# A trunk layer on one core: the first two feed-forward sums taken over the un-normed residual, with the norm brought in where the sums are read

## The chip, the cores and the metric

The kernel runs on one core of a Trainium2 chip. The metric is the device time of one execution in microseconds, the median over a few runs. The profile shows one execution, with its engines named as follows: PE is TensorE's matmul, PEld its weight load, DVE is VectorE, ACT is ScalarE, POOL is GpSimd, SP is SyncE, which issues most of the transfers. "L138" is line 138 of the kernel. The kernel is written in program order: each engine takes its instructions in the order in which the Python code emits them, and waits for others by semaphores that are put in automatically.

## The reference

One layer of a diffusion backbone over 384 tokens (128 of context, 256 latent) of 2048 channels. Token mixing (attention, a Fourier branch, gates) ends in an output projection and a residual; then comes the feed-forward part with which the change deals:

```python
x = x + g1 * token_mixing(h, attn, u, w_na_proj_l, w_fnet_proj_l, w_gate_l, w_o_l)
h2 = rms_norm(x, n2) * (1 + sc2) + sh2
x = x + g2 * swiglu(h2, w_gu_l, w_down_l)

def swiglu(h, w_gate_up, w_down):
    a, g = jnp.split(h @ w_gate_up, 2, axis=-1)
    return (jax.nn.silu(g) * a) @ w_down
```

`rms_norm` divides each token by the root of its mean square over the 2048 channels, so it is one factor per token. `sc2` and `sh2` (scale and shift) are per channel, with one set for the context tokens and another for the latent ones. `D_FF` is 5632.

## The kernel before, in words

**Numbers in two parts.** All matrix products are of fp32 inputs, each split into a high part H, rounded to a shorter format by an ACT copy, and a low part L = x - H by a DVE subtraction (`split`, L135 to L138). `mm3` (L140 to L143) sums three products: H·H, H·L and L·H. So each weight tile costs one ACT cast (L137) and one DVE subtraction (L138).

**Weight units.** Weights stream in units of 256 rows by 512 columns (`load_unit`), issued on SP into four buffers `raw`. `next_unit` is called at the start of each unit's matmuls. It splits one further unit (`split_unit`, into buffers `wh` and `wl`, three of each), then lets the background work in the lists `front` and `behind` advance, starts a further load, and hands out a unit that was split two calls earlier. The split writes into the buffer of the unit just finished, so its cast begins when TensorE has left that unit.

**Background work.** A generator wrapped in `Paced` takes `rate` steps for each `next_unit`, after a delay of `wait` calls. Its instructions stand in the engines' queues behind those of the split in the same call. `rows` is such a generator: it sums the modulation rows of the later gates on DVE (L314), and its rate is set by stage (`RATES`).

**Accumulators.** Matmul outputs go to tiles of one bank in PSUM: four `mm` tiles and three `at` tiles. Sums take them in a ring of seven (`acc_tile`); transposes take an `at` tile.

**Output projection (W_o), L1122 to L1147.** Four chunks of 512 output channels. Each has three sums (one for each 128 tokens) over eight units. At its end x2 = xin + gate · sum is formed per token tile on DVE (L1142, L1143), and its squares are summed per token on ACT (L1145). While a chunk is computed, the chunk before it is turned to channels-first by `transposed` (L1107): for each 128 channels three TensorE transposes into an `at` tile, and two ACT passes that multiply by the scale and store to `x2T`, all in fp32.

**The seam, L1148 to L1187.** The last chunk's squares are summed, the inverse root is taken (`inv_sqrt`, L153), the shift columns `msh[1]` are finished (`rows_until(3)`, with a transpose at L347 and a copy at L351), the inverse is turned and spread over partitions (`rB`, L1157, L1159). `normed` (L1161) makes h2 in steps of two row groups of 128 channels: x2T · rB on DVE (L1165), the high part with the shift added on ACT (L1170), the low part on DVE (L1176). One step is taken ahead of the first feed-forward matmul, and the other seven go on one a unit; the last chunk is transposed in steps 2 to 5. The call of `next_unit` in the last W_o unit leaves out its split (`late`), which is done after the first `normed` step.

**Feed-forward part, L1212 to L1272.** Six parts of 8 or 4 blocks of 128 hidden channels. Per four blocks there are two sums over all 16 row groups, eight units each: first the gate half (`half` = 1), read by a Silu on ACT (L1241), then the linear half, multiplied in by DVE (L1244). The product is split into cH and cL for the down projection (L1251 to L1271), whose results are added up in `facc` until the last part writes y. The accumulators hold 384 tokens as columns, the weights being the stationary side.

Of the kernel before, what the change touches and what calls it, by code (L numbers as in the profile page):

```python
# [19 lines left out]
P = 128  # L20
# [75 lines left out]
def trunk_kernel(ctx: ExitStack, tc: tile.TileContext, io: dict):  # L96
# [28 lines left out]
    dram = ctx.enter_context(tc.tile_pool(name="dram", bufs=1, space=DRAM))  # L125


    small.tile([P, 56], F32, tag="pad", bufs=1, name="pad")

    ids = iter(range(10**9))  # L130

# [67 lines left out]
        for p in front:  # L199
            p.tick()  # L200

    def next_unit(late=False):

        for p in front:
            p.tick()
        if not late:
# [870 lines left out]
    rows_psum["tile"] = lambda: pmd.tile([P, CH], F32, tag="md8", name=nm("md"))  # L1077
    x2p = ctx.enter_context(tc.tile_pool(name="x2p", bufs=1))
    x2 = [x2p.tile([P, NT, CH], F32, tag=f"x2_{i}", name=f"x2_{i}") for i in range(4)]

    gb = [None] * 4

    def load_rows(pool, ty, cc):
        gb[cc] = pool.tile([P, 2, CH], F32, tag=f"gb{cc}", name=nm("gb"))
        for cnd in range(2):
            nc.sync.dma_start(
                gb[cc][:, cnd], s_row[ty][cnd][0, cc * CH : (cc + 1) * CH].partition_broadcast(P)
            )
            yield

    pho = ctx.enter_context(ExitStack())
    xtp = pho.enter_context(tc.tile_pool(name="xtp", bufs=1))
    tmp = pho.enter_context(tc.tile_pool(name="tmpo", bufs=2))
    x2T = [xtp.tile([P, 4, TOK], F32, tag=f"x2T{i}", name=f"x2T{i}") for i in range(4)]
    ssx = small.tile([P, NT, 4], F32, tag="ssx", bufs=1, name="ssx2")

    def load_residual(cc):

        nc.sync.dma_start(xin[cc][:, 0, :], xp[:, cc * CH : (cc + 1) * CH])
        yield  # L1100
        nc.sync.dma_start(
            xin[cc][:, 1:3, :], xs[:, cc * CH : (cc + 1) * CH].rearrange("(t p) d -> p t d", p=P)
        )
        rows_until(2)
        yield from load_rows(xtp, 2, cc)

    def transposed(cc):  # L1107

        for k in range(4):
            kt = cc * 4 + k  # L1110
            o = at_tile()
            for t in range(NT):
                nc.tensor.transpose(o[:, t * P : (t + 1) * P], x2[cc][:, t, k * P : (k + 1) * P], ident)
            for cnd, sl in ((0, slice(0, CTX)), (1, slice(CTX, TOK))):
                nc.scalar.activation(
                    out=x2T[cc][:, k, sl], in_=o[:, sl], func=AF.Copy, scale=msc[1][:, kt, cnd : cnd + 1]
                )
            yield

    rows.rate = RATES[3]  # L1120
    xin = [None] * 4
    for cc in range(4):  # L1122
        xin[cc] = xtp.tile([P, NT, CH], F32, tag="xin", bufs=2, name=nm("xin"))
        behind.append(Paced(load_residual(cc)))
        po = [acc_tile() for _ in range(NT)]
        for u in range(0, KT, 2):
            if cc == 3 and u == KT - 4:
                rows.rate = 0
            if cc == 3 and u == 8:
                warm_sqrt()  # L1130
            wH, wL = next_unit(late=cc == 3 and u == KT - 2)
            if u == 2 and cc:
                rows_until(4)
                behind.append(Paced(transposed(cc - 1)))
            for t in range(NT):
                sl = slice(t * P, (t + 1) * P)
                for kk in range(2):
                    k = u + kk
                    mm3(po[t], mixH[k][:, sl], mixL[k][:, sl], wH[:, kk], wL[:, kk], k == 0, k == KT - 1)
                if u == KT - 2:  # L1140
                    d = tmp.tile([P, CH], F32, tag="d", name=nm("d"))
                    nc.vector.tensor_mul(d, po[t], gb[cc][:, min(t, 1)])  # L1142
                    nc.vector.tensor_add(x2[cc][:, t], xin[cc][:, t], d)  # L1143
                    junk = tmp.tile([P, CH], F32, tag="junk", name=nm("junk"))
                    nc.scalar.activation(  # L1145
                        out=junk, in_=x2[cc][:, t], func=AF.Square, accum_out=ssx[:, t, cc : cc + 1]
                    )  # L1147
    ss2 = small.tile([P, NT], F32, tag="ss1", bufs=1, name="ss2")  # L1148
    nc.vector.tensor_reduce(out=ss2, in_=ssx, axis=AX.X, op=ALU.add)
    r2 = small.tile([P, NT], F32, tag="r1", bufs=1, name="r2")  # L1150
    for _ in inv_sqrt(r2, ss2, D, [P, NT]):
        pass
    rows_until(3)
    last_chunk = transposed(3)
    o = mm_tile()
    for t in range(NT):
        nc.tensor.transpose(o[:, t * P : (t + 1) * P], r2[:, t : t + 1].to_broadcast([P, P]), ident)  # L1157
    rB = tmp.tile([P, TOK], F32, tag="rB", bufs=1, name="rB")
    nc.scalar.copy(rB, o[:, :TOK])  # L1159

    def normed():  # L1161
        for k0 in range(0, KT, 2):
            for kt in (k0, k0 + 1):
                v = x2T[kt // 4][:, kt % 4]
                nc.vector.tensor_mul(v, v, rB)  # L1165
            for kt in (k0, k0 + 1):
                H, L = new_h(kt)
                v = x2T[kt // 4][:, kt % 4]
                for cnd, sl in ((0, slice(0, CTX)), (1, slice(CTX, TOK))):
                    nc.scalar.activation(  # L1170
                        out=H[:, sl], in_=v[:, sl], func=AF.Identity, bias=msh[1][:, kt, cnd : cnd + 1]
                    )
            for kt in (k0, k0 + 1):
                v = x2T[kt // 4][:, kt % 4]
                for cnd, sl in ((0, slice(0, CTX)), (1, slice(CTX, TOK))):
                    nc.vector.scalar_tensor_tensor(  # L1176
                        out=hL[kt][:, sl], in0=v[:, sl], scalar=msh[1][:, kt, cnd : cnd + 1],
                        in1=fr(hH[kt][:, sl]), op0=ALU.add, op1=ALU.subtract,
                    )
            if k0 in (2, 4, 6, 8):  # L1180
                next(last_chunk)
            yield

    norm = Paced(normed())
    norm.step()
    split_unit()
    behind.append(norm)  # L1187


    phf = ctx.enter_context(ExitStack())  # L1190
# [1 line left out]

    def split_act(i, sg, cH, cL):
        for f in range(4):
            split(cH[i + f], cL[i + f], sg[:, f])
            yield

    def gated():

# [1 line left out]
        phr.close()  # L1201
        pool = phr.enter_context(tc.tile_pool(name="gbp", bufs=1, side="right"))
        for cc in range(4):
            yield from load_rows(pool, 5, cc)
        for cc in range(4):
            for t in range(NT):
                v = facc[cc][:, t]
# [5 lines left out]
    for part, nf in enumerate(FF_PARTS):  # L1213
# [5 lines left out]
        for c4 in range(nf // 4):  # L1219
            for half in (1, 0):  # L1220
                po = [acc_tile() for _ in range(4)]
                for u in range(0, KT, 2):
                    wH, wL = next_unit()
                    if u == KT - 2 and facc is None:
                        norm.drain()
                        rows.rate = RATES[4]
                        pho.close()
                        actp = phf.enter_context(tc.tile_pool(name="actp", bufs=1))
                        facc = [actp.tile([P, NT, CH], F32, tag=f"fa{i}", name=f"facc{i}") for i in range(4)]
                        ftmp = phf.enter_context(tc.tile_pool(name="tmpf", bufs=2))  # L1230
                    for f in range(4):
                        s = slice(f * P, (f + 1) * P)
                        for kk in range(2):
                            k = u + kk
                            mm3(po[f][:, :TOK], wH[:, kk, s], wL[:, kk, s], hH[k], hL[k], k == 0, k == KT - 1)
                        if u < KT - 2:
                            continue
                        if half:
                            if f == 0:
                                sg = ftmp.tile([P, 4, TOK], F32, tag="sg", name=nm("sg"))  # L1240
                            nc.scalar.activation(out=sg[:, f], in_=po[f][:, :TOK], func=AF.Silu)  # L1241
                        else:
                            i = c4 * 4 + f
                            nc.vector.tensor_mul(sg[:, f], sg[:, f], po[f][:, :TOK])  # L1244
                            cH[i] = actp.tile([P, TOK], F32R, tag=f"cH{i}", name=nm("cH"))
                            cL[i] = actp.tile([P, TOK], F32R, tag=f"cL{i}", name=nm("cL"))
                            if nf == 4:
                                split(cH[i], cL[i], sg[:, f])
            if nf > 4:
                behind.append(Paced(split_act(c4 * 4, sg, cH, cL), 2))  # L1250
        for cc in range(4):  # L1251
            po = [acc_tile() for _ in range(NT)]
            for u in range(0, nf, 2):
                wH, wL = next_unit()
                for t in range(NT):
# [8 lines left out]
                    elif not last:  # L1264
                        nc.vector.tensor_add(facc[cc][:, t], facc[cc][:, t], po[t])
                    else:
                        d = ftmp.tile([P, CH], F32, tag="d", bufs=1, name=nm("d"))
# [57 lines left out]
```

## Time and profile before

| what | us |
|---|---|
| median of 3 runs | 2071.12 |
| lowest and highest run | 2070.62, 2074.38 |
| the profiled execution, its own time | 2071.76 |
| its span, first to last instruction | 2070.0 |
| TensorE busy in the span | 2035.2 |
| DVE busy | 1225.5 |
| ACT busy | 758.2 |

The page gives busy times over the whole span and per group of instructions; a "tile" name stands for all of its buffers. The views by stretch give the same for chosen times, with the clock that TensorE was granted, 1.00 being full speed; the mean over the span was 0.996. TensorE's busy time contains pipelined matmuls, so "busy" is not "at full rate": the distance from one matmul's start to the next is the better measure. In the timeline, a number in brackets is how long the engine stood idle before an instruction, and after the arrow is whose signal ended it.

### The profile page before, as it was taken

The numbers are of one execution on the slowest core, as the hardware profiler recorded it, in microseconds if no ns is written. First come the engines' busy times: TensorE is split into PE (matmuls) and PEld (weight loads), VectorE is DVE, ScalarE is ACT, GpSimd is POOL, SyncE is SP. The second block draws the span as 40 slices with busy tenths as digits, with TensorE's granted clock in tenths as the row PEclk, the third lists the DMA queues.
The fourth block names the chain that finished last, engine by engine and source line by source line (L and its number), as shares of the span: only waits on it lengthen the run. The fifth ranks groups of instructions, "written<-read, shape, count | busy, mean of one in ns | idle before, by whom it ended". The sixth has DMA issues, their size and how long they took to land.

```text
span 2070.0 us, 27406 instructions
## 1 busy us (share of the span) xinstructions
PE 2035.2 (98%) x10986; PEld 1846.1 (89%) x10986; DVE 1225.5 (59%) x1454; ACT 758.2 (37%) x1133; POOL 43.2 (2%) x92
## 2 busy tenths in 40 slices
PE   7999999999999999998999999999999999999999
PEld 4658888999999999887998899899989998999897
DVE  5635899688986787765554444544454434333456
ACT  5323232456665443334433332223222232223222
POOL 1000000000001000001000000000000000000000
PEclk9999999999999999999999999999999999999999
DMA  9887878677774775754545554455454444444453
GB/s 329 297 318 218 298 247 315 209 211 232 213 223 150 255 245 198 244 182 133 153 153 163 157 159 153 136 160 162 154 163 133 125 130 127 128 126 128 130 166 122
DMA packets 219999, 390.45 MB, mean 189 GB/s; under 512 B 28080, under 2 KB 64960, under 8 KB 219872
## 3 DMA queue, kind: packets, MB, share of 16 engines
q1 hardware_dynamic: 212704, 382.13, 58.2%
q10 hardware_dynamic: 4672, 6.31, 0.8%
q8 instruction: 86, 1.41, 0.3%
q0 software_dynamic: 2496, 0.27, 0.1%
q14 instruction: 41, 0.34, 0.0%
HBM read 371.81 MB, written 20.51 MB: 190 GB/s over the span
## 4 chain that ended last, share of the span: by engine, by line
PE 89%; DVE 3%; DMA 3%; ACT 2%; issue 1%; SPq 1%; ACTq 0%; DVEq 0%
PE mm L141 18%; PE mm L143 18%; PE mm L142 18%; PE at L143 11%; PE at L141 11%; PE at L142 10%; PE md L392 1%; DMA wm<-in_w_mod 1%; DVE accr L314 1%; DMA wraw<-in_w_gate 1%; DVE wl L138 1%; ACT wh L137 0%; ACT sc L900 0%; SPq L368 0%; PE at L858 0%
## 5 line engine op out<-in xcount | busy, mean ns | idle before, releaser
L138 DVE TENSOR_TENSOR wl<-wraw,wh 128x1024 fp32r<-128x1024 f32 (+1 forms) x464 | 559.1, 1205 | 699.9 <-ACT wh L137 693.5
L137 ACT CAST wh<-wraw 128x1024 fp32r<-128x1024 f32 (+1 forms) x464 | 480.6, 1037 | 1030.3 <-PE at L142 283.5
L141 PE MATMUL mm<-hH,wh 128*128 128x384 f32 x1216 | 411.6, 338 | 3.6 <-ACT gst L998 2.5
L143 PE MATMUL mm<-hH,wl 128*128 128x384 f32 x1216 | 407.6, 335 | 0.0
L142 PE MATMUL mm<-hL,wh 128*128 128x384 f32 x1216 | 407.2, 335 | 0.0
L314 DVE SCALAR_TENSOR_TENSOR accr<-wmr,csz,accr 128x1024 f32<-128x1024 f32 x240 | 304.7, 1277 | 0.1
L141 PE MATMUL at<-hH,wh 128*128 128x384 f32 x704 | 236.6, 336 | 1.4 <-ACT hH L1170 1.4
L141 PEld LDWEIGHTS mm<-hH,wh 128*128 128x128 f32 x1216 | 228.9, 188 | 9.2 <-ACT gst L998 3.7
L142 PE MATMUL at<-hL,wh 128*128 128x384 f32 x704 | 236.4, 336 | 0.0
L143 PE MATMUL at<-hH,wl 128*128 128x384 f32 x704 | 235.9, 335 | 0.0
L142 PEld LDWEIGHTS mm<-hL,wh 128*128 128x128 f32 x1216 | 229.0, 188 | 0.0
L143 PEld LDWEIGHTS mm<-hH,wl 128*128 128x128 f32 x1216 | 228.7, 188 | 0.0
L141 PE MATMUL mm<-wh,hH 128*128 128x512 f32 x422 | 168.8, 400 | 1.8 <-DVE gl L1054 1.2
L142 PE MATMUL mm<-wl,hH 128*128 128x512 f32 x422 | 165.0, 391 | 0.9 <-DVE wl L138 0.9
L143 PE MATMUL mm<-wh,hL 128*128 128x512 f32 x422 | 164.7, 390 | 0.0
L143 PE MATMUL mm<-wh,cL 128*128 128x512 f32 x352 | 137.1, 389 | 0.0
L141 PE MATMUL mm<-wh,cH 128*128 128x512 f32 x352 | 137.0, 389 | 0.0
L142 PE MATMUL mm<-wl,cH 128*128 128x512 f32 x352 | 137.0, 389 | 0.0
L141 PEld LDWEIGHTS at<-hH,wh 128*128 128x128 f32 x704 | 132.7, 189 | 2.8 <-ACT hH L1170 1.8
L142 PEld LDWEIGHTS at<-hL,wh 128*128 128x128 f32 x704 | 132.7, 189 | 1.1 <-DVE hL L1176 0.7
L143 PEld LDWEIGHTS at<-hH,wl 128*128 128x128 f32 x704 | 132.7, 189 | 0.0
L141 PEld LDWEIGHTS mm<-wh,hH 128*128 128x128 f32 x422 | 79.5, 188 | 33.7 <-issue 11.1
(239 smaller groups left out, 2390.2 us busy)
## 6 DMA issues: line engine op xcount, KB each, us to landing
wraw<-in_w_gate_up SPq DMA_DIRECT2D x176, 512.0 KB, 3.7
wmr<-in_w_mod SPq DMA_DIRECT2D x128, 512.0 KB, 4.2
wraw<-in_w_down SPq DMA_DIRECT2D x88, 512.0 KB, 3.7
wm<-in_w_mod SPq DMA_DIRECT2D x64, 512.0 KB, 7.1
wraw<-in_w_gate SPq DMA_DIRECT2D x64, 512.0 KB, 5.0
wraw<-in_w_in SPq DMA_DIRECT2D x56, 512.0 KB, 5.8
wraw<-in_w_o SPq DMA_DIRECT2D x32, 512.0 KB, 5.5
wraw<-in_w_fnet_proj SPq DMA_DIRECT2D x16, 512.0 KB, 6.2
```

Of the source, the lines that this page charges most:

```text
L137: nc.scalar.copy(H, x)
L138: nc.vector.tensor_sub(L, x, fr(H))
L141: nc.tensor.matmul(out, aH, bH, start=start, stop=False)
L142: nc.tensor.matmul(out, aH, bL, start=False, stop=False)
L143: nc.tensor.matmul(out, aL, bH, start=False, stop=stop)
L314: nc.vector.scalar_tensor_tensor(out=acc[:, cnd], in0=wm, scalar=sc, in1=acc[:, cnd], op0=ALU.mult, op1=ALU.add)
L392: nc.tensor.matmul(pm[q : q + 32, :w], csz[:, k, :], wm[:, ty, kk + par, :], start=k < 2, stop=k >= KT - 2, tile_position=(0, q), skip_gro ...
```

## The change

The first two feed-forward sums (gate and linear half of the first four blocks) no longer read h2 = x2 · scale · rB + shift. They read x2 · scale alone, with the norm factor rB and the shift brought in when the sums are read. This is possible since rB is one factor per token, that is, per column of the sum, and the shift's contribution is one number per output channel and condition.

- `transposed` now stores x2 · scale split into H and L (two ACT and two DVE passes for each row group) in `xw` (row groups 0 to 11) and `xv` (12 to 15). Their tiles are 386 columns wide: the last two hold the shift of the two conditions (`shifts`), so each sum's columns 384 and 385 come out as the shift's contribution. For this `rows_until(3)` now stands in the last W_o unit.
- The last W_o unit splits a further weight unit as all others do.
- The inverse norm (`inverse`), the transposes of the last chunk and `normed` are all background work in the two sums. `inverse` acts in U0 and U2 (units of these sums, counted from 0), the transposes in U1 to U4, `normed` at 1.25 row groups a unit from the fourth unit on. `normed` adds H and L back together, multiplies by rB and splits into hH and hL, the low part one step behind, for the sums from the third on.
- `late_norm` reads each of the eight accumulators: the two shift columns are copied by ACT, DVE multiplies by rB, and then ACT's Silu takes the shift as its bias (first sum), or DVE adds it and multiplies by the first sum's result (second sum).
- `rows` goes on after the second sum, and not in the last unit of the first. The down projection's tiles are allotted after the second sum too; cH and cL are allotted when they are split. Temporaries `d` and `xin` now serve both stages, and the gate rows `gb` of the projection share two buffers.

```diff
+    XW = TOK + 2
+    xw = [xhp.tile([P, 12, XW], F32R, tag=f"x{n}", name=f"x{n}") for n in "HL"]
...
+    def shifts(some, k0):
+        H, L = some
+        c = slice(k0, k0 + H.shape[1])
+        nc.scalar.copy(H[:, :, TOK:], msh[1][:, c])
+        nc.vector.tensor_sub(L[:, :, TOK:], msh[1][:, c], fr(H[:, :, TOK:]))
...
-            for cnd, sl in ((0, slice(0, CTX)), (1, slice(CTX, TOK))):
-                nc.scalar.activation(
-                    out=x2T[cc][:, k, sl], in_=o[:, sl], func=AF.Copy, scale=msc[1][:, kt, cnd : cnd + 1]
-                )
+            H, L = wide(kt)
+            conds = [(msc[1][:, kt, c : c + 1], sl) for c, sl in ((0, slice(0, CTX)), (1, slice(CTX, TOK)))]
+            for g, sl in conds:
+                nc.scalar.activation(out=H[:, sl], in_=o[:, sl], func=AF.Copy, scale=g)
+            for g, sl in conds:
+                nc.vector.scalar_tensor_tensor(
+                    out=L[:, sl], in0=o[:, sl], scalar=g, in1=fr(H[:, sl]), op0=ALU.mult, op1=ALU.subtract
+                )
...
-            wH, wL = next_unit(late=cc == 3 and u == KT - 2)
+            wH, wL = next_unit()
+            if cc == 3 and u == KT - 2:
+                rows_until(3)
+                shifts(xw, 0)
...
+    def inverse():
+        ss2 = small.tile([P, NT], F32, tag="ss1", bufs=1, name="ss2")
+        nc.vector.tensor_reduce(out=ss2, in_=ssx, axis=AX.X, op=ALU.add)
+        r2 = small.tile([P, NT], F32, tag="r1", bufs=1, name="r2")
+        for _ in inv_sqrt(r2, ss2, D, [P, NT]):
+            pass
+        yield
+        yield
+        o = at_tile()
+        for t in range(NT):
+            nc.tensor.transpose(o[:, t * P : (t + 1) * P], r2[:, t : t + 1].to_broadcast([P, P]), ident)
+        nc.scalar.copy(rB, o[:, :TOK])
...
+        vs = tmp.tile([P, 4, TOK], F32, tag="xin", name=nm("v"))
+        conds = ((0, slice(0, CTX)), (1, slice(CTX, TOK)))
+        for kt in range(KT + 1):
+            if kt < KT:
+                xH, xL = (fr(x[:, :TOK]) for x in wide(kt))
+                v = vs[:, kt % 4]
+                nc.vector.tensor_add(v, xH, xL)
                 nc.vector.tensor_mul(v, v, rB)
+                new_h(kt)
+                for c, sl in conds:
                     nc.scalar.activation(
+                        out=hH[kt][:, sl], in_=v[:, sl], func=AF.Identity, bias=msh[1][:, kt, c : c + 1]
                     )
+            if kt:
+                for c, sl in conds:
                     nc.vector.scalar_tensor_tensor(
+                        out=hL[kt - 1][:, sl], in0=vs[:, (kt - 1) % 4, sl], scalar=msh[1][:, kt - 1, c : c + 1],
+                        in1=fr(hH[kt - 1][:, sl]), op0=ALU.add, op1=ALU.subtract,
                     )
             yield
-    norm = Paced(normed())
-    norm.step()
-    split_unit()
-    behind.append(norm)
+    norm = Paced(normed(), 1.25, 3)
+    behind += [Paced(inverse()), Paced(transposed(3), 1, 1), norm]
...
+    def late_norm(o, sg, half):
+        b = small.tile([P, 2], F32, tag="bias", name=nm("bias"))
+        nc.scalar.copy(b, o[:, TOK:XW])
+        v = sg if half else tmp.tile([P, CH], F32, tag="d", name=nm("v"))[:, :TOK]
+        nc.vector.tensor_mul(v, o[:, :TOK], rB)
+        for c, sl in ((0, slice(0, CTX)), (1, slice(CTX, TOK))):
+            if half:
+                nc.scalar.activation(out=sg[:, sl], in_=v[:, sl], func=AF.Silu, bias=b[:, c : c + 1])
+            else:
+                nc.vector.scalar_tensor_tensor(
+                    out=sg[:, sl], in0=v[:, sl], scalar=b[:, c : c + 1], in1=sg[:, sl], op0=ALU.add, op1=ALU.mult
+                )
...
+                            xH, xL = wide(k) if facc is None else (hH[k], hL[k])
+                            mm3(
+                                po[f][:, : xH.shape[1]], wH[:, kk, s], wL[:, kk, s], xH, xL, k == 0, k == KT - 1
+                            )
...
+                        if facc is None:
+                            late_norm(po[f], sg[:, f], half)
...
+            if facc is None:
+                norm.drain()
+                rows.rate = RATES[4]
+                phx.close()
```

More of the change, by code (lines that the diff above doesn't have):

```diff
@@ L125, in trunk_kernel @@
     dram = ctx.enter_context(tc.tile_pool(name="dram", bufs=1, space=DRAM))
-    small.tile([P, 56], F32, tag="pad", bufs=1, name="pad")
+    small.tile([P, 24], F32, tag="pad", bufs=1, name="pad")
     ids = iter(range(10**9))
@@ L200, in mid_unit, with next_unit @@
             p.tick()
-    def next_unit(late=False):
+    def next_unit():
         for p in front:
             p.tick()
-        if not late:
-            split_unit()
+        split_unit()
         for p in front + behind:
@@ L1079, in trunk_kernel, with load_rows @@
     x2 = [x2p.tile([P, NT, CH], F32, tag=f"x2_{i}", name=f"x2_{i}") for i in range(4)]
+    tmp = ctx.enter_context(tc.tile_pool(name="tmpx", bufs=2))
     gb = [None] * 4
[L1083 to L1084 removed]
+    def load_rows(pool, ty, cc, tag, bufs):
+        gb[cc] = pool.tile([P, 2, CH], F32, tag=tag, bufs=bufs, name=nm("gb"))
         for cnd in range(2):
@@ L1089, in load_rows, with wide @@
             yield
+    XW = TOK + 2
+    phx = ctx.enter_context(ExitStack())
+    xhp = phx.enter_context(tc.tile_pool(name="xhp", bufs=1))
+    xw = [xhp.tile([P, 12, XW], F32R, tag=f"x{n}", name=f"x{n}") for n in "HL"]
+    xv = []
+    def wide(kt):
+        return [x[:, kt] for x in xw] if kt < 12 else [x[:, kt - 12] for x in xv]
+    def shifts(some, k0):
[3 more added lines that the diff above has]
+        nc.vector.tensor_sub(L[:, :, TOK:], msh[1][:, c], fr(H[:, :, TOK:]))
     pho = ctx.enter_context(ExitStack())
-    xtp = pho.enter_context(tc.tile_pool(name="xtp", bufs=1))
-    tmp = pho.enter_context(tc.tile_pool(name="tmpo", bufs=2))
-    x2T = [xtp.tile([P, 4, TOK], F32, tag=f"x2T{i}", name=f"x2T{i}") for i in range(4)]
+    tmpo = pho.enter_context(tc.tile_pool(name="tmpo", bufs=1))
     ssx = small.tile([P, NT, 4], F32, tag="ssx", bufs=1, name="ssx2")
@@ L1104, in load_residual @@
         rows_until(2)
-        yield from load_rows(xtp, 2, cc)
+        yield from load_rows(tmpo, 2, cc, "gb", 2)
     def transposed(cc):
@@ L1122, in trunk_kernel @@
     for cc in range(4):
-        xin[cc] = xtp.tile([P, NT, CH], F32, tag="xin", bufs=2, name=nm("xin"))
+        xin[cc] = tmp.tile([P, NT, CH], F32, tag="xin", name=nm("xin"))
         behind.append(Paced(load_residual(cc)))
@@ L1143, in trunk_kernel @@
                     nc.vector.tensor_add(x2[cc][:, t], xin[cc][:, t], d)
-                    junk = tmp.tile([P, CH], F32, tag="junk", name=nm("junk"))
+                    junk = tmpo.tile([P, CH], F32, tag="junk", name=nm("junk"))
                     nc.scalar.activation(
@@ L1147, in trunk_kernel @@
                     )
[L1148 to L1158, printed above, removed]
@@ L1159, in trunk_kernel @@
-    nc.scalar.copy(rB, o[:, :TOK])
-    def normed():
-        for k0 in range(0, KT, 2):
-            for kt in (k0, k0 + 1):
-                v = x2T[kt // 4][:, kt % 4]
+    pho.close()
+    xvp = phx.enter_context(tc.tile_pool(name="xvp", bufs=1))
+    xv += [xvp.tile([P, 4, XW], F32R, tag=f"v{n}", name=f"v{n}") for n in "HL"]
+    rB = xvp.tile([P, TOK], F32, tag="rB", name="rB")
+    shifts(xv, 12)
+    def inverse():
[10 more added lines that the diff above has]
+        nc.scalar.copy(rB, o[:, :TOK])
@@ L1194, in split_act @@
         for f in range(4):
+            cH[i + f], cL[i + f] = (
+                actp.tile([P, TOK], F32R, tag=f"c{n}{i + f}", name=nm(f"c{n}")) for n in "HL"
+            )
             split(cH[i + f], cL[i + f], sg[:, f])
             yield
+    def late_norm(o, sg, half):
[10 more added lines that the diff above has]
+                )
     def gated():
@@ L1203, in gated @@
         for cc in range(4):
-            yield from load_rows(pool, 5, cc)
+            yield from load_rows(pool, 5, cc, f"gb{cc}", 1)
         for cc in range(4):
@@ L1223, in trunk_kernel @@
                     wH, wL = next_unit()
[L1224 to L1230, printed above, removed]
                     for f in range(4):
@@ L1266, in trunk_kernel @@
                     else:
-                        d = ftmp.tile([P, CH], F32, tag="d", bufs=1, name=nm("d"))
+                        d = tmp.tile([P, CH], F32, tag="d", name=nm("d"))
                         nc.vector.tensor_mul(d, po[t], gb[cc][:, min(t, 1)])
```

31 lines of the change are left out of this document (9 added, 22 removed).

## The prediction

> **What bounds the kernel now.** First the page's busy table: TensorE is busy 98% of the span, so a change can only win where TensorE idles or runs slowly.
>
> ```profile
> PE 2035.2 (98%) x10986; PEld 1846.1 (89%) x10986; DVE 1225.5 (59%) x1454; ACT 758.2 (37%) x1133; POOL 43.2 (2%) x92
> ```
>
> Then the table by stretches across the seam between the output projection and the feed-forward part. Its columns are the stretch, its length, the busy time of PE, PEld, DVE, ACT and POOL, the granted clock, the DMA share and GB/s.
>
> ```profile
> 830.00:958.00 128.00, 128.00 (x586) 104.97 (x585) 80.40 (x77) 46.34 (x74) 5.33 (x11) 1.00 0.64 210
> 958.00:964.00 6.00, 2.42 (x12) 1.80 (x11) 3.85 (x12) 2.37 (x7) 0.00 (x0) 0.92 0.00 0
> 964.00:970.00 6.00, 4.65 (x16) 4.01 (x15) 4.92 (x9) 3.85 (x7) 0.00 (x0) 0.51 0.03 5
> 970.00:980.00 10.00, 9.59 (x57) 8.95 (x56) 7.77 (x16) 6.10 (x14) 0.00 (x0) 1.00 0.52 157
> 980.00:1040.00 60.00, 59.91 (x345) 58.95 (x344) 32.93 (x51) 26.84 (x45) 0.00 (x0) 1.00 0.51 158
> 1040.00:2030.00 990.00, 990.00 (x5270) 931.43 (x5269) 447.90 (x451) 292.49 (x329) 6.26 (x13) 1.00 0.48 144
> ```
>
> TensorE is full up to 958 and again from 980; between, it idles, and runs at a clock of 0.51. The timeline says for what; brackets give the idle time ahead of an instruction and what ended it.
>
> ```profile
> 951.05 0.39 PE L141 MATMUL mm<-wh,hH 128*128 128x512 f32 x1
> ...
> 955.13 0.39 PE L141 MATMUL mm<-wh,hH 128*128 128x512 f32 x1
> ...
> 958.05 0.69 DVE L1142 TENSOR_TENSOR d<-mm,gb 128x512 f32<-128x512 f32 x1
> ...
> 960.92 0.63 ACT L1145 ACTIVATE junk<-x 128x512 f32<-128x512 f32 x1 [0.70 <-DVE x L1143]
> ...
> 961.67 0.17 DVE L1149 TENSOR_REDUCE ss<-ssx 128x3 f32<-128x12 f32 x1 [0.85 <-ACT junk L1145]
> ...
> 962.08 0.20 ACT L157 ACTIVATE rss<-rsv 128x3 f32<-128x3 f32 x1 [0.43 <-DVE rsv L155]
> ...
> 963.13 0.90 PE L1157 MATMUL mm<-ident,r 128*128 128x128 f32 x3 [3.58 <-DVE r L162]
> ...
> 966.02 0.69 PE L141 MATMUL at<-hH,wh 128*128 128x384 f32 x1 [1.35 <-ACT hH L1170]
> ```
>
> A W_o unit takes 4.08 (first two rows), so the projection ends at 959.2. TensorE then waits for the inverse norm and the first normed row. I call the feed-forward units of 24 matmuls U0, U1, and so on: the first two sums are U0 to U15, the third starts with U16. ACT's weight casts mark them, about 0.2 after each unit's start:
>
> ```profile
> 1024.75 1.05 ACT L137 CAST wh<-wraw 128x1024 fp32r<-128x1024 f32 x1 [3.11 <-PE at L142]
> ...
> 1037.23 1.05 ACT L137 CAST wh<-wraw 128x1024 fp32r<-128x1024 f32 x1 [3.11 <-PE at L142]
> ...
> 1045.59 1.05 ACT L137 CAST wh<-wraw 128x1024 fp32r<-128x1024 f32 x1 [2.28 <-issue]
> ```
>
> Three units fill 12.48, so a steady one takes 4.16; U16 starts at 1037.05, U18 at 1045.4. From 959.2 to 1045.4 are 86.2 us for 18 units worth 74.9: 11.3 us of other things. Four groups of three transposes stay. Such a group stretches a W_o unit from 4.08 to 4.45:
>
> ```profile
> 868.58 1.05 ACT L137 CAST wh<-wraw 128x1024 fp32r<-128x1024 f32 x1 [2.77 <-PE at L143]
> ...
> 873.03 1.05 ACT L137 CAST wh<-wraw 128x1024 fp32r<-128x1024 f32 x1 [2.77 <-PE at L143]
> ```
>
> So 0.37 a group, 1.5 for four, and 0.5 at that rate for rB's three and the shift's one. **At most 9.3 us (0.45%) can be won.**
>
> **The change, part by part.** *The gap.* U0 needs only x2 without its norm and the shift columns, so the waits of 3.58 and 1.35 and the slow clock behind them go. The shift's transpose moves ahead of the last W_o unit, which starts at 955.1. Its input is issued on POOL at 949.34 and 0.5 later, and lands in time (at most 3.7 later):
>
> ```profile
> 949.34 0.99 POOL L340 DMA_DIRECT2D colr<-s_row x2 [1.88 <-DMA s_row<-row]
> ```
>
> ```profile
> DMA to landing us min/median/max: 2.0/2.8/3.7
> L1086 SPq DMA_DIRECT2D gb<-s_row x16: 338/464/929, 834.1 to 1984.9; - x16
> ```
>
> Behind that unit's weights (low part done 2.5 after its start, at 957.6, by the cast rows below) come three tiny operations of 0.2: columns ready at 958.2. The three x2 tiles follow, six DVE passes of 0.69: 962.3, ahead of U1's transposes at 963.4. SP's order stays. The row sums of type 5 restart 8 units (33 us) later and are first read near 1985: no cost; if they came late, DVE would pay 1.28 a step there.
>
> *386 columns.*
>
> ```profile
> L143 PE MATMUL mm<-hH,wl 128*128 128x384 f32 x1216 | 407.6, 335 | 0.0
> ...
> L143 PE MATMUL mm<-wh,cL 128*128 128x512 f32 x352 | 137.1, 389 | 0.0
> ...
> L143 PE MATMUL at<-AH,chanL 128*128 128x388 f32 x16 | 5.4, 340 | 0.0
> ```
>
> That is 0.4 ns a column from 384 to 512 and 1.2 from 384 to 388: two columns in 384 matmuls cost 0.3 to 1.0 us. I take 0.4 (units of 4.18), the longer lever.
>
> *In W_o* DVE makes 12 low parts of 0.79 under a full TensorE (DVE 80.4 of 128 busy). In its second chunk two of three `at` tiles hold sums, so the third is freed by DVE, behind a row sum, instead of ACT; TensorE may wait 0.3 in three units: 0 to 1 us, I take 0.3.
>
> *The helpers' ring.* This decides, I expect. Each unit of the two sums issues a weight cast (ACT) and low part (DVE), then 1.25 steps of the norm: add and multiply on DVE, two ACT passes, and the low part of the row before, two DVE passes. Before, in DVE's and in ACT's timeline:
>
> ```profile
> 975.74 1.58 DVE L1176 SCALAR_TENSOR_TENSOR hL<-x2T,msh,hH 128x128 fp32r<-128x128 f32 x4
> 978.38 1.23 DVE L138 TENSOR_TENSOR wl<-wraw,wh 128x1024 fp32r<-128x1024 f32 x1 [1.06 <-ACT wh L137]
> 979.53 1.02 DVE L1165 TENSOR_TENSOR x2T<-x2T,rB 128x384 f32<-128x384 f32 x2
> ```
>
> ```profile
> 972.50 1.04 ACT L137 CAST wh<-wraw 128x1024 fp32r<-128x1024 f32 x1
> 975.30 1.50 ACT L1170 ACTIVATE hH<-x2T,msh 128x128 fp32r<-128x128 f32 x4 [1.76 <-DVE x2T L1165]
> 976.71 0.71 ACT L1115 ACTIVATE x2T<-at,msc 128x128 f32<-128x128 f32 x2
> 977.32 1.04 ACT L137 CAST wh<-wraw 128x1024 fp32r<-128x1024 f32 x1
> ```
>
> Each queue keeps its order, so the work forms a ring: cast to low part 1.06, low part 1.15, add and multiply 1.02, over to ACT 0.07, two ACT passes 0.70 (half of 1.41), and only then the next cast: **4.00 us for a unit with one step**. Every fourth unit has two; the second adds 0.79 (half of 1.58) and 1.02: **5.81**. Four units of ring take 17.8, of TensorE 16.7, so the helpers lose 1.1 each time. Their cover is the weights' lead: unit n's cast serves n+2, 8.36 later, and is done with its low part in 2.29, so 6.1 us of lag are free. Beyond that TensorE waits.
>
> *One `at` tile in U1 and U2.* Two hold sums again; row 12's transposes, rB's and row 13's share the third. After x2 (962.3) come the square and the spare shift columns (1.0), U2's cast and low part (2.3), the small inverse (1.4, as from 961.67 to 963.1 before), U3's low part (1.2) and row 12's (0.8): the tile is free at 969.0, TensorE there at 968.0. rB's transposes and its ACT copy (0.5) then hold up row 13's. With rB's own 0.4 this costs 2.0.
>
> *Summing the ring.* U6 starts at 959.2 + 6 x 4.18 + 1.5 + 2.0 = 987.8; its cast is at 988.5, as row 15's passes lengthened the units before. U6 has two steps: U7's cast at 994.3, its ring done at 998.3. Then the late norm of the first sum: per accumulator a tiny ACT copy, a DVE multiply, two Silu passes. ACT and DVE don't read one accumulator at once, as the attention part shows:
>
> ```profile
> 529.93 0.37 ACT L875 ACTIVATE sc<-at,rq 128x128 f32<-128x128 f32 x1 [3.67 <-DVE sc L870]
> ...
> 1000.72 1.28 ACT L1241 ACT_TABLE_LOAD   x1
> ...
> 1036.36 0.56 DVE L1244 TENSOR_TENSOR sg<-sg,at 128x384 f32<-128x384 f32 x1
> ```
>
> ACT is held for 0.1 + table load 1.28 + Silu 0.70, then three times 0.25 + 0.58 + 0.70: 6.7 us (the copy as L157's 0.20, the multiply from the last row with its hand-over, Silu as the L1170 passes). U8's cast comes at 1005.0, 8.8 after its unit's start at 996.2: 2.7 us of stall at U10. From there the ring sets the pace: U8 and U9 4.00 each, U10 5.81, U11 to U13 4.00 each, U14 5.81, U15 4.00, to 1040.6. Then the late norm of the second sum, on DVE in front of the next weights: 0.25, four times 0.51 + 0.79, the last row's low part 0.79, the weights' 1.23. U18 can start at **1048.1**, though TensorE ended U17 at 1043.1. Against 1045.4 that loses **2.7 us**: the gain at the head is taken back.
>
> *The clock.* The last stall is 5.0 us. A shorter one dropped the clock before:
>
> ```profile
> 648.50 0.44 PE L141 MATMUL mm<-hH,wh 128*128 128x384 f32 x1 [2.20 <-ACT gst L998]
> ...
> 650.00:652.00 2.00, 2.00 (x8) 2.00 (x7) 0.00 (x0) 1.20 (x4) 1.24 (x3) 0.50 0.55 200
> 652.00:654.00 2.00, 2.00 (x13) 2.00 (x12) 1.79 (x2) 1.92 (x5) 1.71 (x5) 0.90 0.30 106
> ```
>
> After 2.20 idle TensorE ran at half speed until about 652.4, 3.9 after its restart; at the seam from 966.0 until about 970. I take 3.8 us at half speed, **1.9 lost** (0 to 1.9). After U10 a drop only uses up waits that the ring imposes later anyway. The Trainium skill, "TensorE: Matmul & The Clock Gate", Part 1, says that the clock drops after a whole idle window of about 3.4 us on a free-running grid. By it the 2.20 would not have dropped it, which the row at 650 contradicts; a 5.0 us stall would hold a whole window only about every second time, and the term would be an estimated 0.9.
>
> **Sum:** 2.7 + 0.3 (W_o) + 1.9 = +4.9 on the profiled run of 2071.76 (span 2070.0), which lies 0.6 above the median 2071.12: **2076.0 us**, 0.24% slower. A measurement of this kernel can tell about 0.2%, 4.1 us, from no change.
>
> **Rivals.**
> 1. *The ring with a warm clock, or a shorter ring.* Without the drop 2071.1 + 3.0 = 2074.1; if ACT's copy did not hold DVE either, three hand-overs of 0.8 would go, 2071.7. Against: the rows at 529 and 650. For: each 1% of a 60 us ring is 0.6. Not measurable.
> 2. *Faster: the lead covers it.* If casts overlapped the norm's passes, DVE's work a unit (1.15 + 1.25 x 1.81 = 3.4) would stay under 4.18, and TensorE would keep 9.3 less 1.6 (the `at` tile) and 0.7 (columns, W_o): 7.0, 2064.1. It turns where the ring's mean falls below 4.18; I have 4.45. For: DVE was busy only 32.93 of 60 after 980. Against: the casts at 972.50 and 977.32, 4.82 apart, are such a ring.
> 3. *The gap stays in part:* U0 or row 12 still waits, though shift columns and x2 have margins of about 1 us. A miss of 2 gives 2078.0.
>
> **How the numbers follow.** Forecast 0.50, rival 1 0.32, rival 2 0.13, rival 3 0.05. The range leaves out rival 2 and the far end of 3: 2069 to 2080. Faster by over 0.2% 0.13, within 0.32, slower 0.55.
>
> **What would show it.** Right: no wait for r or hH near 959; short waits at rB's and row 13's transposes; waits for weight low parts (L138) at U10 and, near 5 us, at U18, with a clock near 0.5 behind it; casts 4.0 and 5.8 apart. Wrong: U16 reached near 1030 with the casts still waiting for TensorE, or a wait at U18 under 2 us.

## The result, and the profile after

The changed kernel takes 2075.05 us (median of 16 runs, 2073.54 to 2076.95), the kernel before in the same comparison 2070.90 (16 runs, 2068.51 to 2074.38). The ratio is **1.0021, with a 95% interval of 1.0014 to 1.0028: 4.2 us slower**, just at the 0.2% that I had named as the limit of what can be told, but with a sign that the interval settles. The forecast was 2076.0 with a range of 2069 to 2080.

The profiled execution of the changed kernel took 2074.58, with a span of 2072.8, which is only 2.8 more than the span before. That pair of spans understates it, since the two executions reach the changed part at different times. In ACT's timeline, the cast that follows a pair of casts at the start of W_o can serve as a mark that both kernels have, and the cast of U19, the second of the steady units behind the seam, as the end. Before:

```profile
831.53 1.06 ACT L137 CAST wh<-wraw 128x1024 fp32r<-128x1024 f32 x1 [0.87 <-ACT wh L137]
...
1049.71 1.05 ACT L137 CAST wh<-wraw 128x1024 fp32r<-128x1024 f32 x1 [3.06 <-PE mm L142]
```

After:

```profile
829.96 1.06 ACT L137 CAST wh<-wraw 128x1024 fp32r<-128x1024 f32 x1 [0.86 <-ACT wh L137]
...
1052.87 1.05 ACT L137 CAST wh<-wraw 128x1024 fp32r<-128x1024 f32 x1 [3.06 <-PE mm L142]
```

From mark to U19 it took 218.18 before and takes 222.91 after: **4.7 us more inside the changed stretch**, and the mark itself came 1.57 earlier in that execution, ahead of anything discussed here. Below, "after the mark" is a time counted from there; the same is done for each experiment.

The table by stretches of the changed kernel, with the columns of the prediction's:

```profile
958.00:964.00 6.00, 6.00 (x36) 5.81 (x35) 4.04 (x8) 3.32 (x8) 0.00 (x0) 1.00 0.32 89
964.00:970.00 6.00, 5.05 (x30) 4.52 (x30) 4.71 (x11) 3.39 (x7) 0.00 (x0) 1.00 0.53 146
...
980.00:1040.00 60.00, 54.15 (x301) 52.55 (x299) 42.52 (x78) 27.08 (x56) 0.00 (x0) 0.99 0.35 98
1040.00:1060.00 20.00, 18.94 (x96) 18.94 (x97) 14.19 (x25) 7.40 (x14) 0.00 (x0) 0.85 0.58 207
```

The hole between 958 and 970 is gone, with its slow clock. Another one has opened later: between 980 and 1040 TensorE is busy 54.15 of 60, and from 1040 the clock is 0.85. TensorE's timeline says for what it waits there:

```profile
1004.15 0.34 PE L143 MATMUL at<-xH,wl 128*128 128x386 f32 x1
1005.17 0.44 PE L141 MATMUL mm<-xH,wh 128*128 128x386 f32 x1 [0.68 <-ACT wh L137]
...
1006.43 0.44 PE L143 MATMUL mm<-xH,wl 128*128 128x386 f32 x1 [0.64 <-DVE wl L138]
...
1041.06 0.69 PE L141 MATMUL mm<-hH,wh 128*128 128x384 f32 x1 [4.80 <-DVE v L1234]
...
1046.03 0.37 PE L141 MATMUL mm<-hH,wh 128*128 128x384 f32 x1
...
1048.69 0.33 PE L141 MATMUL at<-hH,wh 128*128 128x384 f32 x1
```

The waits of 0.68 and 0.64 are U10's, and both releasers are the weight split. The one of 4.80 is in U16, the first unit of the third sum, and its releaser is the late norm of the second sum (L1234). At 1046.03 the full speed is back (below). The last row is U18's first matmul. ACT's timeline shows what made the split late:

```profile
996.81 0.80 ACT L1203 ACTIVATE hH<-v,msh 128x128 fp32r<-128x128 f32 x2 [2.35 <-DVE v L1200]
997.52 0.14 ACT L1232 COPY bias<-at 128x2 f32<-128x2 f32 x1
...
1003.38 0.80 ACT L1237 ACTIVATE sg<-sg,bias 128x128 f32<-128x128 f32 x2 [0.62 <-DVE sg L1234]
1004.09 1.03 ACT L137 CAST wh<-wraw 128x1024 fp32r<-128x1024 f32 x1
1007.47 0.81 ACT L1203 ACTIVATE hH<-v,msh 128x128 fp32r<-128x128 f32 x2 [2.35 <-DVE v L1200]
1008.18 1.03 ACT L137 CAST wh<-wraw 128x1024 fp32r<-128x1024 f32 x1
...
1012.27 1.03 ACT L137 CAST wh<-wraw 128x1024 fp32r<-128x1024 f32 x1
...
1017.38 0.80 ACT L1203 ACTIVATE hH<-v,msh 128x128 fp32r<-128x128 f32 x2 [0.92 <-DVE v L1200]
1018.09 1.03 ACT L137 CAST wh<-wraw 128x1024 fp32r<-128x1024 f32 x1
```

From 997.52 to 1004.09 the first late norm holds ACT. From 978 until the second late norm no cast waits for TensorE any more. Outside the late norm each stands behind an `hH` pass, which waited for DVE (2.35 in a single step): casts come 4.09 apart with one norm step between them, and 5.82 with two. ACT is busy 27.08 of 60 here, and DVE 42.52: neither is full, and yet the pair of them sets the pace. DVE's end of it, at the second sum's late norm:

```profile
1039.45 0.74 DVE L1208 SCALAR_TENSOR_TENSOR hL<-v,msh,hH 128x128 fp32r<-128x128 f32 x2
1040.45 0.56 DVE L1234 TENSOR_TENSOR v<-mm,rB 128x384 f32<-128x384 f32 x1 [0.25 <-ACT bias L1232]
...
1046.12 1.22 DVE L138 TENSOR_TENSOR wl<-wraw,wh 128x1024 fp32r<-128x1024 f32 x1
```

The first multiply there starts at 1040.45, only when the ring has let go of DVE and, 0.25 later, of ACT, whose bias copy stood behind the last `hH` pass. It frees the accumulator at which TensorE stands. The last row is the low part of U18's weights: done at 1047.34, some 1.3 before TensorE gets there.

### The profile page after: what moved, and what is told of

It is laid out like the page before. It is cut to its first block, busy times and chain, and to the rows that moved or that the text cites. A ratio compares the mean times of both kernels' runs of the same rounds, so it can differ in the third digit from the quotient of the medians.

```text
span 2072.8 us, 27495 instructions
## 1 busy us (share of the span) xinstructions
PE 2037.9 (98%) x10986; PEld 1847.2 (89%) x10986; DVE 1247.5 (60%) x1516; ACT 760.8 (37%) x1147; POOL 43.3 (2%) x92
## 4 chain that ended last, share of the span: by engine, by line
PE 89%; DVE 4%; ACT 2%; DMA 2%; issue 1%; SPq 1%; ACTq 0%; DVEq 0%
PE mm L141 19%; PE mm L142 18%; PE mm L143 18%; PE at L143 10%; PE at L141 10%; PE at L142 10%; PE md L391 1%; DMA wm<-in_w_mod 1%; DVE accr L313 1%; DVE wl L138 1%; ACT wh L137 1%; PE at L857 1%; PE at L925 0%; SPq L181 0%; PE at L947 0%
## 5 line engine op out<-in xcount | busy, mean ns | idle before, releaser
L138 DVE TENSOR_TENSOR wl<-wraw,wh 128x1024 fp32r<-128x1024 f32 (+1 forms) x464 | 559.3, 1206 | 682.7 <-ACT wh L137 681.6
L141 PE MATMUL mm<-hH,wh 128*128 128x384 f32 x1152 | 390.4, 339 | 7.8 <-DVE v L1234 4.8
L143 PE MATMUL mm<-hH,wl 128*128 128x384 f32 x1152 | 386.0, 335 | 0.0
L142 PE MATMUL mm<-hL,wh 128*128 128x384 f32 x1152 | 385.8, 335 | 0.0
L142 PEld LDWEIGHTS mm<-hL,wh 128*128 128x128 f32 x1152 | 216.8, 188 | 0.0
L143 PE MATMUL at<-hH,wl 128*128 128x384 f32 x640 | 214.2, 335 | 0.0
L141 PE MATMUL at<-hH,wh 128*128 128x384 f32 x640 | 214.2, 335 | 0.0
L142 PE MATMUL at<-hL,wh 128*128 128x384 f32 x640 | 214.2, 335 | 0.0
L141 PEld LDWEIGHTS at<-hH,wh 128*128 128x128 f32 x640 | 120.4, 188 | 0.2
L142 PEld LDWEIGHTS at<-hL,wh 128*128 128x128 f32 x640 | 120.4, 188 | 0.2
L143 PEld LDWEIGHTS at<-hH,wl 128*128 128x128 f32 x640 | 120.4, 188 | 0.0
```

Of the source, the lines that this page charges most:

```text
L138: nc.vector.tensor_sub(L, x, fr(H))
L141: nc.tensor.matmul(out, aH, bH, start=start, stop=False)
L142: nc.tensor.matmul(out, aH, bL, start=False, stop=False)
L143: nc.tensor.matmul(out, aL, bH, start=False, stop=stop)
```

## The experiments

My theory: the helpers' ring (weight cast on ACT, low part, add and multiply on DVE, high part on ACT, next cast), together with the late norm in the same two queues, falls behind TensorE and hands back what the seam had won. Rivals: the 386 columns, the `at` tiles, the clock after the stall, or DVE simply having too much work. Experiments 1 to 4 share runs of the kernel before (2071.33, 22 runs), and 5 to 8 others (2070.99, 23 runs); with the 2070.90 of the first comparison these differ by 0.4, so the difference of two medians from separate comparisons is uncertain by about as much. All start from the changed kernel.

### 1. The high part one step behind

```diff
+            if kt:
                 for c, sl in conds:
                     nc.scalar.activation(
-                        out=hH[kt][:, sl], in_=v[:, sl], func=AF.Identity, bias=msh[1][:, kt, c : c + 1]
+                        out=hH[kt - 1][:, sl], in_=vs[:, (kt - 1) % 4, sl], func=AF.Identity,
+                        bias=msh[1][:, kt - 1, c : c + 1],
                     )
-            if kt:
```

> The high part of each normed row is written one step later too, beside its low part, so that ACT's two passes stand right behind the weight cast and wait for nothing, and the next cast no longer waits for DVE's multiply. Ring theory: the casts again start when TensorE leaves a unit (4.2 us apart), the waits near 1005 and 1019 go, DVE reaches the second sum's first accumulator about 8 us earlier and the 4.8 us wait at the third sum's first unit shrinks below 1 us; time about 2065.5 (2063 to 2068), 9 to 10 below the changed kernel and 5 below the one before. Rival (the 386 columns, the late norm's own work or a slower DVE and ACT cost the time, not the order of the queues): same amount of work, so it stays within 2 us of 2075.

Measured: **2065.01** (5 runs, 2063.77 to 2066.39), ratio 0.9968 [0.9956, 0.9981]. The two waits that TensorE has between 955 and 1062, and its row for the stretch that had the hole:

```profile
PE at L1129 <- ACT rB L1189: 0.6, 1, 0.6
PE at L1188 <- DVE vL L1135: 0.4, 1, 0.4
```

```profile
980.00:1040.00 60.00, 60.00 (x342) 60.00 (x341) 51.14 (x97) 33.81 (x70) 0.00 (x0) 1.00 0.40 112
```

ACT's and DVE's timelines in one of these units:

```profile
1017.99 1.05 ACT L137 CAST wh<-wraw 128x1024 fp32r<-128x1024 f32 x1 [0.98 <-ACT hH L1204]
...
1019.07 0.80 ACT L1204 ACTIVATE hH<-v,msh 128x128 fp32r<-128x128 f32 x2
1019.61 1.22 DVE L138 TENSOR_TENSOR wl<-wraw,wh 128x1024 fp32r<-128x1024 f32 x1
```

The high part now starts right behind the cast, with no wait, since its input was made a step before, and DVE's low part of the weights doesn't wait either. The work is the same, and DVE does more of it in the stretch than in the change (51.14 busy for 42.52), under a full TensorE. So DVE did not have too much to do: it was the order that made two engines with time to spare take turns. There is little room to spare, though: behind the first late norm DVE shows no idle time from 1003.61 to 1022.5 while it catches up. By the medians this one move is worth 10.0 us against the changed kernel, and makes it 0.32% faster than the kernel before.

### 2. The low part in its own step

```diff
-            if kt:
+            if kt < KT:
                 for c, sl in conds:
                     nc.vector.scalar_tensor_tensor(
-                        out=hL[kt - 1][:, sl], in0=vs[:, (kt - 1) % 4, sl], scalar=msh[1][:, kt - 1, c : c + 1],
-                        in1=fr(hH[kt - 1][:, sl]), op0=ALU.add, op1=ALU.subtract,
+                        out=hL[kt][:, sl], in0=v[:, sl], scalar=msh[1][:, kt, c : c + 1],
+                        in1=fr(hH[kt][:, sl]), op0=ALU.add, op1=ALU.subtract,
                     )
```

> Undoes one part: each low part stands in the step of its own row again, behind the high part that it needs. Ring theory: a unit with one step stays at 4.09 (the low part is done before the next cast is), a unit with two steps grows from 5.8 to about 6.6, since the second add waits for the first low part and that for ACT; three such units, so U16 and the time come 2.4 us later, 2077.5 (2076 to 2079). Rival (DVE's and ACT's amount of work decides): no difference, 2075.

Measured: 2077.66 (6 runs, 2076.82 to 2079.41), ratio 1.0029 [1.0018, 1.0041]. A double step in ACT's timeline:

```profile
1012.90 1.03 ACT L137 CAST wh<-wraw 128x1024 fp32r<-128x1024 f32 x1
1016.28 0.80 ACT L1203 ACTIVATE hH<-v,msh 128x128 fp32r<-128x128 f32 x2 [2.35 <-DVE v L1200]
1018.70 0.80 ACT L1203 ACTIVATE hH<-v,msh 128x128 fp32r<-128x128 f32 x2 [1.62 <-DVE v L1200]
1019.41 1.03 ACT L137 CAST wh<-wraw 128x1024 fp32r<-128x1024 f32 x1
```

The second `hH` pass waits 1.62 instead of 0.92, and the double step takes 6.51 instead of 5.82; a single one stays at 4.10. So the ring is lengthened by 0.7 in each fourth unit, which is 2.1 in the three double steps. TensorE's restart in U16 comes 213.5 after the mark for the change's 211.1, and the time follows, by 2.6. The part of the change that puts the low part a step behind does help; it is the other pass, the high part, that closes the ring.

### 3. The bias copy on DVE

```diff
-        nc.scalar.copy(b, o[:, TOK:XW])
+        nc.vector.tensor_copy(b, o[:, TOK:XW])
```

> The copy of the two shift columns in the late norm goes from ACT to DVE, so that ACT's Silu passes of one accumulator run beside DVE's multiply of the next. Ring theory: ACT is held 4.2 instead of 6.6 us behind the first sum, the wait near 1005 goes, the whole ring behind it and the second sum's late norm come 2.4 us earlier, and the wait at the third sum shrinks from 4.8 to about 2.4: time 2072 (2070.5 to 2073.5). Rival (ACT and DVE may read one accumulator at once, the hand-over costs nothing): 2075 to 2075.5.

Measured: 2073.12 (11 runs, 2071.67 to 2074.87), ratio 1.0009 [1.0000, 1.0017], 1.9 less than the change. ACT's timeline at the first late norm:

```profile
997.54 0.80 ACT L1203 ACTIVATE hH<-v,msh 128x128 fp32r<-128x128 f32 x2 [2.35 <-DVE v L1200]
...
999.64 2.88 ACT L1237 ACTIVATE sg<-sg,bias 128x128 f32<-128x128 f32 x8
1002.43 1.03 ACT L137 CAST wh<-wraw 128x1024 fp32r<-128x1024 f32 x1
```

The eight Silu passes run without a break, and the cast follows the `hH` pass by 4.89 instead of 7.28: 2.4 less, as worked out. Besides the 0.4 and 0.6 near 969, which stay, the list of TensorE's waits has only these two left:

```profile
PE mm L141 <- DVE v L1234: 4.6, 1, 4.6
PE mm L143 <- DVE wl L138: 0.5, 1, 0.5
```

The waits at U10 are gone; the 0.5 is U13's. But the one at U16 stayed at 4.6, where I had expected 2.4: TensorE, no longer held at U10, came to that point 2.4 earlier after the mark, and the late norm that it waits for there came 2.6 earlier (208.5 after the mark, for 211.1). The late norm pushes the whole ring back, wherever TensorE then pays for it.

### 4. No shift columns

The matmuls read 384 columns, and the bias is taken from the sum's first two, so this kernel leaves the shift out of its first two sums.

```diff
-        return [x[:, kt] for x in xw] if kt < 12 else [x[:, kt - 12] for x in xv]
+        return [x[:, kt, :TOK] for x in xw] if kt < 12 else [x[:, kt - 12, :TOK] for x in xv]
...
-        nc.scalar.copy(b, o[:, TOK:XW])
+        nc.scalar.copy(b, o[:, 0:2])
```

> Leaves out the shift in the first two sums: the matmuls read 384 columns instead of 386, and the bias copy reads two other columns of the same accumulator, so every wait stays. Ring theory: TensorE saves 0.3 to 1.0 us in units that wait for the ring anyway, so the time stays within 0.7 of the changed kernel, 2075. Rival (386 columns, not a multiple of 32, are read or written slowly): 2 us or more are saved, 2073 or less.

Measured: 2074.89 (11 runs, 2072.56 to 2077.64), ratio 1.0018 [1.0009, 1.0027]. That can't be told from the change. The columns do slow TensorE a little: 133 matmuls in a row take 23.39 from first to last start after, 0.1772 each, and 23.22 without the columns, 0.1759 each. In TensorE's timeline, first and last of the 133 after,

```profile
979.70 0.33 PE L143 MATMUL at<-xH,wl 128*128 128x386 f32 x1
...
1003.09 0.34 PE L143 MATMUL at<-xH,wl 128*128 128x386 f32 x1
```

and without the columns:

```profile
979.69 0.34 PE L143 MATMUL at<-xH,wl 128*128 128x384 f32 x1
...
1002.91 0.34 PE L143 MATMUL at<-xH,wl 128*128 128x384 f32 x1
```

That is 0.5 us in 384 matmuls. While the ring sets the pace it is waited away: no difference shows in the time.

### 5. Experiments 1 and 3 together

> Both edits of the runs e1 and e3 together. Ring theory: a hand-over between ACT and DVE costs only inside the ring; with the ring broken no wait for weights is left for it to shorten, so the time stays with e1, 2065.0 (2064 to 2066). Rival (the hand-overs cost 1.9 by themselves, as e3 gained): 2063.

Measured: 2064.92 (6 runs, 2062.78 to 2067.31), ratio 0.9971 [0.9959, 0.9983]: the same as experiment 1. The copy on ACT cost 1.9 while the ring was closed, and nothing that can be measured once it is open.

### 6. rB's transposes in their own bank, on top of experiment 1

```diff
-        o = at_tile()
+        o = rows_psum["tile"]()
```

> The edit of e1, and the transposes of the inverse norm go to the bank of the row sums, which rest at that time, so that they no longer share the one free accumulator bank with rows 12 and 13. Theory (one bank in the first units costs two waits): the waits of 0.4 and 0.6 us near 969 go, 1 us less than e1, 2064.0 (2063 to 2065). Rival (those waits are covered by slack later): 2065.

Measured: 2064.52 (6 runs, 2063.09 to 2065.92), ratio 0.9970 [0.9957, 0.9982]. The two waits of experiment 1, 1.0 together, are gone from the trace: TensorE has none left between 950 and 1062. By time the step from experiment 1, 0.5, isn't separable from nothing, since the intervals overlap almost wholly.

### 7. The wait at U16 filled with matmuls

22 further matmuls into a bank at rest, in front of the fourth accumulator's first matmul in U16. They keep TensorE busy in front of the wait and add nothing to the sums.

```diff
+                            if part == 0 and c4 == 1 and half and k == 0 and f == 3:
+                                extra = rows_psum["tile"]()
+                                for _ in range(22):
+                                    nc.tensor.matmul(extra[:, :TOK], wH[:, kk, s], xH, start=True, stop=True)
```

> The changed kernel with 22 extra matmuls (3.8 us, into the resting bank of the row sums, read by nobody) in front of the matmul that waits 4.8 us in U16, so that TensorE idles there only about 1 us. Clock theory: the clock stays at full speed behind the wait; half of what the drop costs (16 matmuls at 0.32 instead of 0.17, 2.3 us) comes back, since U18's weights come at 1047.4 anyway where TensorE now starts U18 at 1048.5: 1.2 us less, 2073.8 (2073 to 2074.7). Rival 1 (the drop costs its full 2.3): 2072.7. Rival 2 (the clock does not matter behind this wait): 2075.

Measured: 2073.84 (10 runs, 2071.82 to 2075.02), ratio 1.0014 [1.0004, 1.0023]. By time alone that overlaps with the change; the trace tells them apart. Its timeline and, behind it, its table by stretches:

```profile
1037.73 3.98 PE L1277 MATMUL md<-hH,wh 128*128 128x384 f32 x22
1042.71 0.44 PE L141 MATMUL mm<-hH,wh 128*128 128x384 f32 x1 [1.00 <-DVE v L1234]
...
1048.03 0.33 PE L141 MATMUL at<-hH,wh 128*128 128x384 f32 x1
...
1049.04 0.44 PE L143 MATMUL at<-hH,wl 128*128 128x384 f32 x1 [0.50 <-DVE wl L138]
```

```profile
1041.00:1045.00 4.00, 3.00 (x18) 2.68 (x17) 3.67 (x10) 1.98 (x7) 0.00 (x0) 1.00 0.46 131
```

The same stretch of the changed kernel, which lies at its restart:

```profile
1036.00:1041.00 5.00, 0.26 (x2) 0.00 (x0) 3.57 (x7) 2.65 (x9) 0.00 (x0) 0.83 0.27 64
1041.00:1045.00 4.00, 3.94 (x12) 3.94 (x13) 3.86 (x11) 0.75 (x2) 0.00 (x0) 0.50 0.14 53
```

At the full clock the way from the accumulator's release to U18's first matmul takes 5.32 instead of 7.63. Of these 2.3, about 0.8 goes to a new wait for U18's low weights: 0.50 idle by the row at 1049.04, and more by the distance between the starts, since that matmul starts 0.84 behind the one before it. The mark and U19 in ACT's timeline give the balance:

```profile
831.61 1.06 ACT L137 CAST wh<-wraw 128x1024 fp32r<-128x1024 f32 x1 [0.85 <-ACT wh L137]
...
1052.99 1.05 ACT L137 CAST wh<-wraw 128x1024 fp32r<-128x1024 f32 x1 [2.89 <-PE mm L142]
```

That is 221.38 for the change's 222.91. So between these two executions the slow clock costs some 1.5 of the change's time, and the rest of it would be lost to the weights anyway.

### 8. A free fourth accumulator for the third sum

```diff
+                if part == 0 and c4 == 1 and half:
+                    po = [acc_tile() for _ in range(3)] + [rows_psum["tile"]()]
+                else:
                     po = [acc_tile() for _ in range(4)]
```

> The changed kernel, with the third sum's fourth accumulator in the resting bank of the row sums, so that U16 need not wait for the second sum's late norm. DVE theory (the late norm and the weights stand in one queue): TensorE goes on through U17 and then waits about 5 us at U18 for its low weights, which come at 1047.4 as before, and the clock drops there: the time stays, 2075.5 (2074 to 2077). Rival (holding the accumulators is the cause): 4 us or more are saved, 2071 or less.

Measured: 2075.90 (10 runs, 2074.88 to 2080.27), ratio 1.0027 [1.0018, 1.0036]. TensorE's timeline:

```profile
1049.53 0.67 PE L143 MATMUL at<-hH,wl 128*128 128x384 f32 x1 [4.42 <-DVE wl L138]
1050.00 0.52 PE L141 MATMUL at<-hH,wh 128*128 128x384 f32 x1
```

With the accumulator free, the long wait moves to U18 and its low weights, at 4.42, and the half clock (0.52 for a matmul) goes with it. So what TensorE waits for at U16 is not the accumulator as such. Both waits are for the same backlog on DVE, and whichever TensorE meets first takes it all.

## Why the prediction was right

The sum was +4.9; measured were +4.2 by the runs, and +4.7 from the mark to U19. The ring's length, the late norm and the lost lead came out as forecast; the place of the long wait did not. The steps that carry the sum:

- **The gap goes, and the lead is then lost in the ring.** Shown. With the ring opened (experiment 1) the same kernel is 6.3 faster than before instead of 4.2 slower; with the ring lengthened (experiment 2) it is 6.3 slower than before. That is also rival 2 (2064.1) found as a kernel: its condition, casts that overlap the norm's passes, is just what experiment 1 makes.
- **The ring's length**, 4.00 for a single step and 5.81 for a double: 4.09 and 5.82.
- **ACT held 6.7 by the first late norm:** from 997.52, when the last `hH` pass ends, to 1004.09 are 6.6. That ACT and DVE take turns at an accumulator is part of it: the copy moved away gave 2.4 in ACT's row and 1.9 in the time.
- **U18 at 1048.1, and 1.9 lost to the clock behind its start:** with a unit of 4.16 that puts U19 at 1054.2, which is 222.6 after the mark of before (831.53), or 222.9 with the 0.3 of W_o. Measured: U19's first matmul at 1052.85, 222.9 after the mark. U18 itself came at 218.7 instead of 216.6, since the slow stretch lay in front of it and not behind.
- **The `at` tile in U1 and U2** was put at 2.0, 0.4 of it for rB's own transposes. The two waits, 1.6 of it, came where I had them, but are only the 0.4 and 0.6 of experiment 1's rows, which stand in the change's list too. While the ring is closed they should cost nothing in the end, since TensorE later waits for the helpers anyway; no run tests that.

Three things were off, none of them by much in the sum:

- **The step "U18 can start at 1048.1, though TensorE ended U17 at 1043.1" put the long wait at the wrong place.** I took TensorE to run through U16 and U17, and to stand at U18 for the low weights (L138). It stood at U16 for the late norm's multiply (L1234). What I had missed is the ring of seven accumulators, of which each sum takes four: the third sum's fourth is the twelfth taken, and so the same as the fifth, the second sum's first, which the late norm still held. The size came out right all the same (4.80 for 5.0), because both waits hang on the same DVE backlog; experiment 8 gives my place for it, 4.42 at U18, with no time gained.
- **The stall at U10** was 1.3 idle (0.68 and 0.64) instead of 2.7, and a smaller one, 0.8, followed at U13. The helpers were about where I had them: the cast of 1004.09 is 174.1 after the mark, predicted 173.5. But TensorE came later, at 1004.3, which is 174.4 for a predicted 173.0. The matmuls of these two sums start 0.1772 apart, 4.25 a unit, not 4.18; and a wait in W_o was larger than thought, as TensorE's timeline has it:

```profile
867.48 0.52 PE L1129 MATMUL at<-ident,x 128*128 128x128 f32 x3 [0.52 <-DVE xL L1135]
```

  I had 0.3 for W_o in all. Of what the sums lose a unit, the columns are 0.03 (experiment 4); why matmuls over 384 of these tiles' columns still start 0.1759 apart, where the third sum's are at 0.173, stays open. By this account none of it is in the final time: it only took from waits that the ring imposed. For the two columns experiment 4 shows that.
- **The clock** was 0.50 for longer than the 3.8 taken: 15 matmuls of the sum take the 4.97 from 1041.06 to 1046.03, for 2.60 at 0.1733 each: 2.4 lost. But about 0.8 of that stands in the shadow of U18's weights, and 1.5 is what filling the wait gave back in the trace, for the 1.9 of the sum; the medians differ by 1.2, with intervals that overlap. The other 3.2 of the 4.7 are the ring and W_o, put at 3.0. That the clock's term came so near is partly luck: the sum had no such shadow in it, and the slow stretch is of no fixed length (last section).

Rival 1 (no drop of the clock, 2074.1) lies close to what experiment 7 makes of the kernel, 2073.84, and is ruled out for the change itself by the row of 0.50 from 1041. Its other half, that ACT's copy does not hold DVE, is ruled out by experiment 3, which moves that copy and gains 1.9. Rival 3 (a gap left at the head) is ruled out by the row of 958 to 964.

**What beats both kernels** is experiment 1, alone or with 3 or 6: 2064.5 to 2065.0, which these runs can't rank. It wins some 6 us of the 9.3 that the seam had to give. By an estimate from the rows above, the other 3 are the longer units (4.25 for 4.16 in sixteen units, 1.4), the two waits at the `at` tile (1.0) and the wait in W_o (0.5).

## What to carry to other kernels

When work is moved into the background of a full engine, its busy time isn't what must fit: draw the chain that runs back and forth between the helper engines in one round, hand-overs included, and compare its length with the round of the engine that it serves. If the chain is the longer one, look for the pass that closes it, and issue that pass one round later from data already there; here that took no instruction away and was worth 10 us. And before an accumulator's wait is treated by another buffer, see what its releaser itself was behind: if that is a backlog, the wait will only move.

## What was not expected of the hardware

The length of the slow clock after a stall varied. After 4.80 idle the clock was 0.50 for 4.97 (1041.06 to 1046.03), or 15 matmuls. In experiment 4 about the same wait, 4.90, cost less, as TensorE's timeline shows at its restart:

```profile
1040.02 0.69 PE L141 MATMUL mm<-hH,wh 128*128 128x384 f32 x1 [4.90 <-DVE v L1234]
...
1042.99 0.33 PE L141 MATMUL at<-hH,wh 128*128 128x384 f32 x1
```

Full speed was back after 3.0, or 9 matmuls. In the traces of the other experiments it took 3.4 after the 4.42 of experiment 8 (10 matmuls), and 5.9 after the 4.63 of experiment 3 and the 5.9 of experiment 2 (18 each). Each is one execution, so a difference of a microsecond between two of these profiles can be the clock's alone.

The Trainium skill, "TensorE: Matmul & The Clock Gate", Part 1, says that the window by which the clock rises is about 3.4 us and runs freely, and that the turn therefore varies by some 0.5 us. These rows agree that it varies after much the same stall, but 3.0 to 5.9 lie further apart than that. The Trainium skill also counts, in the same part, 6, 11 or 14 slow matmuls for one kernel in different runs; here they are 9 to 18. The rule that the prediction quotes from the same page of the Trainium skill made a drop after 5.0 us likely only about every second time; all five stalls of 4.42 to 5.9 in these traces were followed by one.

Short waits left the clock alone: the 1.00 in experiment 7 did (the row at 1041 has 1.00), while the 2.20 that the prediction quotes had dropped it.
